# Reordering a hybrid encoder step: group A's prompt attention beside group B's projection, decode beside group B's attention, output projection 512 wide

## The chip, the cores and the metric

The kernel runs on one core of a Trainium2 chip, as one launch. The metric is the device time of that launch in microseconds. Each of the core's engines works through a queue of its own in order: TensorE (PE, matmuls and transposes; weight loads are PEld), VectorE (DVE), ScalarE (ACT), GpSimd (POOL) and SyncE (SP, which here issues every DMA). They wait for each other by semaphores.

## The reference

One layer of an encoder, for a prompt of 1024 tokens and for 8 decode sequences of 16 new tokens with caches. Half of the 16 heads (group A) use stick-breaking attention over the whole past, half (group B) softmax attention over a band of 8 chunks of 64 with a relative bias.

```python
def stick_breaking(q, k, v, q_pos, k_pos):
    z = jnp.einsum('bqhd,bkhd->bhqk', q, k).astype(jnp.float32) * (HEAD_DIM ** -0.5)
    causal = k_pos[None, :] < q_pos[:, None]
    log_keep = jnp.where(causal, jax.nn.log_sigmoid(-z), 0.0)
    between = lax.cumsum(log_keep, axis=3, reverse=True) - log_keep
    w = jnp.where(causal, jnp.exp(jax.nn.log_sigmoid(z) + between), 0.0)
    return jnp.einsum('bhqk,bkhd->bqhd', w.astype(v.dtype), v)

def trunk_layer(x, p, ...):
    h = rmsnorm(x, g_mix)
    q_a, k_a, v_a, q_b, k_b, v_b = split_heads(h, w_in)
    ...
    a = rmsnorm(a, g_out_sb.reshape(N_HEADS_SB, HEAD_DIM))
    o_b = rmsnorm(o_b, g_out_cb.reshape(N_HEADS_CB, HEAD_DIM))
    mix = jnp.concatenate([a.reshape(b, t, W_SB), o_b.reshape(b, t, W_CB)], axis=-1)
    x = x + mix @ w_out
    h = rmsnorm(x, g_ffn)
    x = x + (jax.nn.silu(h @ w_gate) * (h @ w_up)) @ w_down
    gate = jax.nn.sigmoid(rmsnorm(x, g_ple) @ w_ple_gate)
    x = x + gate * (p @ w_ple_proj)
    return x, new
```

The model width is 1024, a head has 64 dimensions, the past is 1024 tokens for group A and 512 for group B in decode. All data are float32. The new keys and values are outputs too.

## The kernel before

**Precision and tiles.** A float32 operand is split into a high and a low part in a reduced type: ACT copies the high part, and DVE (or POOL, where the source is in SBUF) subtracts it for the low part (`sub`, L108). A product is then three matmuls, `mm3` (L103 to L106). Prompt and decode tokens form nine tiles of 128 rows, eight for the prompt and one for the 128 decode tokens.

**Stages.** The program is written as generators, each `yield` being one step, and `advance(main, side, ratio, steps)` runs a main generator with `ratio` steps of a side one after each of its own. `schedule_with_timeline_sim` then orders the instructions on each engine. The order in the program is its priority, so an instruction that finds its inputs and a buffer free can be placed ahead of earlier ones.

1. The norm and transposes of x give `hT`.
2. `qkv_group(0)` (L211): group A's k, v and q by w_in, six weight chunks in 48 steps; the results go to DRAM (`qkT`, `vhl`) and to the outputs.
3. `qkv_group(1)` beside `decode` at 0.8 decode steps a step.
4. `attention` over eight head pairs, four of group A and then four of group B. A unit is one head and one tile of 128 queries: `scores` (L537), five units later `flip` (transposes the weights, L576), one further `outputs` (L597), and after each pair `finish` (L622). That makes 64 units for each group. For group A, `scores` has two sigmoids on ACT, a scan on DVE (L569) and a product on POOL (L570). Beside the first 64 units run `embed` (L751, the per-layer embedding, 18 steps) at 0.5 and decode at 0.4; beside the next 48, decode at 0.7; beside the rest, `half_out` at 1.5.
5. `half_out` (L828): `mix` (L807) loads group A's attention output back from DRAM and transposes it, then the first 512 rows of w_out are applied, 256 columns at a time. `lower` (L870) applies group B's half together with the next norm.
6. The feed-forward part, the per-layer gate and the final norm.

**Decode.** There are 16 batches (8 sequences, group A and then group B), with 4 chunks of 256 past tokens for group A and 2 for group B, each once for k and once for v: 96 steps and one to set up. A chunk of 512 KB is loaded into a raw tile `draw` (L131 to L134), of which there are two (`RAWS`). `fetch(i + 2)` is asked for once step i is under way and needs a raw tile that is free again. A k chunk is transposed by PE (L367) and split by ACT (L369) and DVE; a v chunk is copied by ACT (L148) and subtracted by POOL (L109), and the raw tile is free when the last reader has ended.

**Buffers.** PSUM has eight banks. In stages 1 to 3 the right side holds decode's (`d` = 2, `a` = 1), the left side `t` = 2, `o` = 2 and `s` = 1; in stage 4 the left side has `s` = 2 and `t` = 3. `half_out`'s `m` = 2 takes the place of `d` and `a`, after decode. Weights go through `Chunks`, one raw tile (`wraw`) and two pairs (`whi`, `wlo`); attention's tiles for q, k and v carry these same tags, and `finish` uses `wraw`.

Of the kernel before, what the change touches and what calls it, by code (L numbers as in the profile page):

```python
# [13 lines left out]
F32 = mybir.dt.float32  # L14
F32R = mybir.dt.float32r
# [7 lines left out]
P = 128  # L23
D = 1024
KT = 8
NP = 8
NT = 9
HD = 64
# [4 lines left out]
N4, SKEW = 14, 3  # L33
LAG, RAWS, PT = 5, 2, 2


@with_exitstack
def tile_hymba_step(
# [172 lines left out]
    def qkv_group(grp, ch, hT, stg, pso, pst):  # L211
        def parts(n, src, scale=1.0):
            hl = [stg.tile([P, 384], F32R, name=f"st{x}", tag=f"st{x}")[:, :n] for x in "hl"]
# [13 lines left out]
        for i, (w, c) in enumerate(order):  # L227
# [16 lines left out]
                for g in range(3):  # L244
# [14 lines left out]
                    else:  # L259
                        sv = stg.tile([P, 12, 2, HD], F32R, name="sv", tag="sv", bufs=1)  # L260
                        flat = st.rearrange("p t (h d) -> p (t h) d", d=HD)
                        A.copy(sv[:, :, 0, :], flat)
                        sub(G, sv[:, :, 1, :], flat, sv[:, :, 0, :])
                        nc.sync.dma_start(
                            vhl[grp][c, g * 384 : (g + 1) * 384, :].rearrange("(t p) n -> p t n", p=P),
                            sv.bitcast(F32).rearrange("p (t h) x d -> p t (h x d)", t=3),
                        )
# [230 lines left out]
    def attention(qp, ap_, ps, lag):  # L498
# [7 lines left out]
        def head(st, hh):  # L506
# [5 lines left out]
            qk = qp.tile([P, 2 * D], F32R, name="qk", tag="whi", bufs=2)  # L512
            vk = qp.tile([P, 2 * D], F32R, name="vk", tag="wlo", bufs=2)
# [16 lines left out]
        def bias(st, hh):  # L530
            toep = ap_.tile([P, (7 + hh) * P], F32, name="toep", tag=f"keep{2 + hh}")[:, :640]
# [5 lines left out]
        def scores(st, hh, t):  # L537
# [6 lines left out]
            if not grp:  # L544
                keep = ap_.tile([P, (5 + t % 4) * P], F32, name="keep", tag=f"keep{t % 4}")[:, :n]
# [51 lines left out]
        def outputs(st, hh, g, wt):  # L597
# [20 lines left out]
            tmp = ap_.tile([P, 256], F32, name="obt", tag="obt", bufs=2)  # L618
# [174 lines left out]
    for _ in dec:  # L793
        pass
# [245 lines left out]
```

## Time and profile before

| | us |
|---|---|
| median of 3 runs | 1923.72 |
| lowest and highest run | 1920.15, 1925.52 |
| the profiled execution | 1920.99 |
| its span, first to last instruction | 1919.2 |
| PE busy in it | 1833.9 (96%) |
| PEld busy | 1733.7 (90%) |
| DVE, POOL, ACT busy | 823.2, 722.3, 718.2 |
| mean granted TensorE clock | 0.991 |

The profile is of one execution. Its page gives the busy time of each engine, then the span in 40 equal slices of 48 us, where a digit is the busy share in tenths. Tables by stage give, for a stretch A:B, its length and the busy time and number of instructions of each engine, followed by the granted TensorE clock, the busy share of the DMA engines and GB/s. Rows by line or tile give an engine's operation, out<-in, its count, the least, median and greatest duration in ns, and the first and last start. A timeline row gives start and duration in us, and in brackets the idle time before it and what ended it. Matmuls overlap in the pipeline, so a busy PE isn't yet a PE at its peak; the distance between the starts of two matmuls is the better measure.

### The profile page before, as it was taken

To read this page: it belongs to the slowest core of one execution; us is meant where nothing else is said; L and a number is where in the kernel's file an instruction comes from. 1 tells how busy PE (TensorE), PEld (TensorE's weight loads), DVE (VectorE), ACT (ScalarE), POOL (GpSimd) and SP (SyncE) were. 2 spreads that over 40 slices of the span, in tenths; PEclk is the share of its full clock that TensorE was granted. 3 is DMA by queue.
4 is the path that set the end of the run, shared out by engine and by line. 5 is a ranking of instruction groups with operands and counts; after the bars stand their busy time and mean duration, and the time that the engine had idled before them with its cause. 6 is when DMAs were issued, how large, how long until landed. Compare 5 with 4: busy or idle time off the path is not lost.

```text
span 1919.2 us, 30012 instructions
## 1 busy us (share of the span) xinstructions
PE 1833.9 (96%) x11998; PEld 1733.7 (90%) x11998; DVE 823.2 (43%) x1590; ACT 718.2 (37%) x1545; POOL 722.3 (38%) x600
## 2 busy tenths in 40 slices
PE   7999999988888798899999999999999999999998
PEld 7999999987777688889999999999999999999898
DVE  5201332347888888783541331321322312313735
ACT  5322444347778687872241111111111111121532
POOL 4232345446567744523022223223223223122355
PEclk9999999999999899999999999999999999999999
DMA  6555556576558576773011111111111101111133
GB/s 214 201 176 177 183 192 203 172 229 184 161 144 218 150 223 196 214 234 117 12 45 45 44 44 44 44 45 44 45 44 44 44 29 38 44 45 44 36 98 132
DMA packets 166011, 220.60 MB, mean 115 GB/s; under 512 B 14576, under 2 KB 118768, under 8 KB 165872
## 3 DMA queue, kind: packets, MB, share of 16 engines
q1 hardware_dynamic: 165872, 218.69, 37.2%
q8 instruction: 95, 1.56, 0.4%
q14 instruction: 44, 0.36, 0.1%
HBM read 168.84 MB, written 49.81 MB: 114 GB/s over the span
## 4 chain that ended last, share of the span: by engine, by line
PE 61%; DVE 5%; DMA 3%; ACT 3%; POOL 2%; issue 1%; SPq 0%; POOLq 0%; ACTq 0%; DVEq 0%
PE ps L104 16%; PE ps L105 16%; PE ps L106 16%; PE acc L104 2%; PE acc L106 2%; DVE keep L569 2%; PE acc L105 2%; DMA draw<-in_cache_cb_v 1%; PE pt L589 1%; DVE wtl L109 1%; PE pt L613 1%; PE pt L187 1%; PE pt L612 1%; PE pt L367 1%; ACT dhi L148 1%
## 5 line engine op out<-in xcount | busy, mean ns | idle before, releaser
L109 POOL TENSOR_TENSOR wlo<-wraw,whi 128x1024 fp32r<-128x1024 f32 (+1 forms) x118 | 257.2, 2200 | 605.1 <-ACT whi L148 605.1
L106 PE MATMUL ps<-hUh,wlo 128*128 128x384 f32 x1056 | 352.9, 334 | 0.0
L104 PE MATMUL ps<-hUh,whi 128*128 128x384 f32 x1056 | 352.9, 334 | 0.0
L105 PE MATMUL ps<-hUl,whi 128*128 128x384 f32 x1056 | 352.9, 334 | 0.0
L148 ACT CAST whi<-wraw 128x1024 fp32r<-128x1024 f32 (+1 forms) x118 | 107.6, 962 | 328.0 <-PE ps L106 227.4
L923 DVE TENSOR_TENSOR x<-x,ps 128x512 f32<-128x512 f32 x198 | 135.9, 687 | 158.3 <-PE ps L106 158.3
L104 PEld LDWEIGHTS ps<-hUh,whi 128*128 128x128 f32 x1056 | 198.2, 188 | 0.4
L105 PEld LDWEIGHTS ps<-hUl,whi 128*128 128x128 f32 x1056 | 198.2, 188 | 0.4
L106 PEld LDWEIGHTS ps<-hUh,wlo 128*128 128x128 f32 x1056 | 198.2, 188 | 0.0
L104 PE MATMUL ps<-whi,hTh 128*128 128x256 f32 x576 | 165.4, 287 | 0.7 <-ACT sth L215 0.6
L105 PE MATMUL ps<-wlo,hTh 128*128 128x256 f32 x576 | 164.6, 286 | 1.0 <-POOL wlo L109 1.0
L106 PE MATMUL ps<-whi,hTl 128*128 128x256 f32 x576 | 165.0, 287 | 0.0
L109 POOL TENSOR_TENSOR dlo<-draw,dhi 128x1024 fp32r<-128x1024 f32 x48 | 117.8, 2455 | 102.1 <-ACT dhi L148 95.3
L105 PE MATMUL ps<-wlo,acth 128*128 128x512 f32 x396 | 156.2, 394 | 0.0
L104 PE MATMUL ps<-whi,acth 128*128 128x512 f32 x396 | 155.3, 392 | 0.0
L106 PE MATMUL ps<-whi,actl 128*128 128x512 f32 x396 | 153.8, 388 | 0.0
L909 DVE TENSOR_TENSOR tmp<-sg,ps 128x384 f32<-128x384 f32 x66 | 36.6, 555 | 235.4 <-PE ps L106 235.4
L907 DVE TENSOR_TENSOR sg<-tmp,ps 128x384 f32<-128x384 f32 x66 | 36.5, 554 | 197.7 <-ACT tmp L906 197.7
L109 POOL TENSOR_TENSOR actl<-tmp,acth 128x384 fp32r<-128x384 f32 x66 | 66.5, 1007 | 133.8 <-ACT acth L910 133.8
L105 PEld LDWEIGHTS ps<-wlo,hTh 128*128 128x128 f32 x576 | 111.0, 193 | 1.3 <-POOL wlo L109 1.3
L104 PEld LDWEIGHTS ps<-whi,hTh 128*128 128x128 f32 x576 | 111.0, 193 | 1.1 <-ACT sth L215 0.8
L569 DVE TENSOR_TENSOR_SCAN keep<-keep,zero 128x128 f32<-128x128 f32 (+3 forms) x64 | 105.7, 1658 | 14.1 <-ACT keep L561 11.0
(187 smaller groups left out, 4439.4 us busy)
## 6 DMA issues: line engine op xcount, KB each, us to landing
draw<-in_cache_sb_k SPq DMA_DIRECT2D x32, 512.0 KB, 4.4
draw<-in_cache_sb_v SPq DMA_DIRECT2D x32, 512.0 KB, 3.9
wraw<-in_w_in SPq DMA_DIRECT2D x12, 1024.0 KB, 5.5
wraw<-in_w_gate SPq DMA_DIRECT2D x11, 1024.0 KB, 5.4
wraw<-in_w_up SPq DMA_DIRECT2D x11, 1024.0 KB, 5.5
wraw<-in_w_down SPq DMA_DIRECT2D x11, 1024.0 KB, 4.9
v<-sv SPq DMA_DIRECT2D x12, 768.0 KB, 4.1
x<-in_x_prompt SPq DMA_DIRECT2D x16, 512.0 KB, 6.4
```

Source lines behind the costliest of these rows:

```text
L104: T.matmul(out, lhsT=ah, rhs=bh, start=start, stop=False)
L105: T.matmul(out, lhsT=ah, rhs=bl, start=False, stop=False)
L106: T.matmul(out, lhsT=al, rhs=bh, start=False, stop=stop)
L109: eng.tensor_tensor(out, a, hi.bitcast(F32), op=ALU.subtract)
L148: A.copy(h[:, o], v[:, o])
L187: T.transpose(pt[:, j * P : (j + 1) * P], h[:, c : c + P], ident)
L367: T.transpose(pt[:, pr * P : (pr + 1) * P], raw[:, m, pr * P : (pr + 1) * P], ident)
L569: V.tensor_tensor_scan(rev, rev, zero[:, 0:1].to_broadcast([P, n]), 1.0, op0=ALU.mult, op1=ALU.add)
L589: T.transpose(pt[:, (c - c0) * P : (c - c0 + 1) * P], w[:, c * P : (c + 1) * P], ident)
L907: V.tensor_tensor(out[0][:, f, s], t_, ps, op=ALU.mult)
L909: V.tensor_tensor(t_, sg[:, f, s], ps, op=ALU.mult)
L923: V.tensor_tensor(x1[t][:, o], x1[t][:, o], ps, op=ALU.add)
```

## The change

Stage 2 stays. Group A's attention now runs beside `qkv_group(1)`, at `QA` = 1.2 of its steps a projection step. Decode starts after that projection, since its pool `dA` and its banks now take the right side that the projection has left, and runs beside the next 48 attention steps at `DEC` = 2.0, with `embed` at 0.4. What is then left of attention runs with `half_out` at `OUT` = 1.0.

```diff
-N4, SKEW = 14, 3
+SKEW = 3
 LAG, RAWS, PT = 5, 2, 2
+QA, DEC, OUT = 1.2, 2.0, 1.0
...
-    banks(right, "right", d=2, a=1)
-    banks(left, "left", t=2, o=2, s=1)
+    banks(left, "left", s=2, t=3)
+    banks(right, "right", o=3)
     ch = Chunks(pool(ctx, "w1", "left"), "w", 2048, 1, 2)
-    hp = pool(left, "h1", "left")
-    stg = pool(left, "stg", "left", 2)
+    hp = pool(right, "h1", "right")
+    stg = pool(right, "stg", "right", 2)
...
+    at = pool(left, "at", "left")
+    att = attention(ch.pool, at, ps, LAG)(range(8))
+
+    advance(qkv_group(1, ch, hT, stg, ps["o"], ps["t"]), att, QA)
+    right.close()
     dstack = ExitStack()
+    banks(dstack, "right", d=2, a=1)
     dp = pool(dstack, "dA", "right")
     dec = decode(Chunks(dp, "d", 1088, RAWS, 2, 1024), dp)
-    advance(qkv_group(1, ch, hT, stg, ps["o"], ps["t"]), dec, 0.8)
-
-    left.close()
-    banks(left, "left", s=2, t=3)
-    at = pool(left, "at", "left")
-    att = attention(ch.pool, at, ps, LAG)(range(8))
...
     pj = embed()
-    advance(both(att, pj, 4, 0.5), dec, 0.4, 4 * 2 * NP)
+    advance(both(att, pj, 0, 0.4), dec, DEC, 48)
     for _ in pj:
         pass
-    pstack.close()
-    advance(att, dec, 0.7, 48)
     for _ in dec:
         pass
+    pstack.close()
     dstack.close()
-    right.close()
...
     side = half_out()
-    advance(att, side, 1.5, N4)
-    w_b = [upper(ch, 0, 512)]
-    advance(att, side, 1.5)
+    advance(att, side, OUT)
     left.close()
```

The output projection works on 512 columns throughout, and its weights all come through `ch`; the pool `wA` is gone:

```diff
-        for c in range(4):
-            wh, wl = wp.load(w_out[0, :512, c * 256 : (c + 1) * 256].rearrange("(k p) c -> p k c", p=P), 4, 256)
+        for c in range(2):
+            wh, wl = out_weights(0, c)
...
-                acc = ps["m"].tile([P, 256], F32, name="acc", tag="M")
+                acc = ps["m"].tile([P, 512], F32, name="acc", tag="M")
...
+    def out_weights(grp, c):
+
+        return ch.load(w_out[0, grp * 512 : grp * 512 + 512, c * 512 : (c + 1) * 512].rearrange("(k p) c -> p k c", p=P),
+                       4, 512)
...
-    w_b += [upper(wp, c, 256) for c in (2, 3)]
+    w_b = [out_weights(1, c) for c in range(2)]
...
-        for n, w in (((512, w_b[0]),), ((256, w_b[1]), (256, w_b[2])))[half]:
-            o = slice(0, 512) if n == 512 else slice(256 * (w is w_b[2]), 256 * (w is w_b[2]) + 256)
-            for k in range(4):
-                mm3(acc[:, o], *hT.tok(t, 4 + k), w[0][:, k], w[1][:, k], k == 0, k == 3)
+        for k in range(4):
+            mm3(acc, *hT.tok(t, 4 + k), w_b[half][0][:, k], w_b[half][1][:, k], k == 0, k == 3)
```

Since attention's tiles and the projection's now live at the same time, buffers are cut or moved: attention's q, k and v get tiles of their own in `at`, and v's split is stored a token tile at a time.

```diff
-            hl = [stg.tile([P, 384], F32R, name=f"st{x}", tag=f"st{x}")[:, :n] for x in "hl"]
+            hl = [stg.tile([P, 384], F32R, name=f"st{x}", tag=f"st{x}", bufs=1 + (x == "h"))[:, :n] for x in "hl"]
...
-                        sv = stg.tile([P, 12, 2, HD], F32R, name="sv", tag="sv", bufs=1)
...
+                        for o in range(3):
+                            sv = stg.tile([P, 4, 2, HD], F32R, name="sv", tag="sv", bufs=2)
...
-            qk = qp.tile([P, 2 * D], F32R, name="qk", tag="whi", bufs=2)
-            vk = qp.tile([P, 2 * D], F32R, name="vk", tag="wlo", bufs=2)
+            qk = ap_.tile([P, 2 * D], F32R, name="qk", tag="qk", bufs=2)
+            vk = ap_.tile([P, 2 * D], F32R, name="vk", tag="vk", bufs=2)
...
-                keep = ap_.tile([P, (5 + t % 4) * P], F32, name="keep", tag=f"keep{t % 4}")[:, :n]
+                keep = ap_.tile([P, (7, 8, 6)[t % 3] * P], F32, name="keep", tag=f"keep{t % 3}")[:, :n]
...
-            tmp = ap_.tile([P, 256], F32, name="obt", tag="obt", bufs=2)
+            tmp = ap_.tile([P, 256], F32, name="obt", tag="obt", bufs=1)
```

`bias` in group B's attention takes its tile from two of the three keep tags, `embed` loads w_ple_proj as one chunk through `ch` in place of two through a pool of its own, and the program reserves less memory for dynamic DMA descriptors (`dynamic_dma_scratch_size=1024`).

More of the change, by code (lines that the diff above doesn't have):

```diff
@@ L259, in qkv_group @@
                     else:
-                        sv = stg.tile([P, 12, 2, HD], F32R, name="sv", tag="sv", bufs=1)
[L261 to L267, printed above, removed]
+                        for o in range(3):
+                            sv = stg.tile([P, 4, 2, HD], F32R, name="sv", tag="sv", bufs=2)
+                            flat = st[:, o].rearrange("p (h d) -> p h d", d=HD)
+                            A.copy(sv[:, :, 0, :], flat)
+                            sub(G, sv[:, :, 1, :], flat, sv[:, :, 0, :])
+                            tok = slice((g * 3 + o) * P, (g * 3 + o + 1) * P)
+                            nc.sync.dma_start(vhl[grp][c, tok, :], sv.bitcast(F32).rearrange("p h x d -> p (h x d)"))
                     first = 4 if grp else 0
@@ L530, in bias @@
         def bias(st, hh):
-            toep = ap_.tile([P, (7 + hh) * P], F32, name="toep", tag=f"keep{2 + hh}")[:, :640]
+            toep = ap_.tile([P, (8 - hh * 2) * P], F32, name="toep", tag=f"keep{1 + hh}")[:, :640]
             nc.sync.dma_start(toep, rel[st["pr"] * 2 + hh])
@@ L751, in embed @@
     def embed():
-        wc = Chunks(pp, "p", 1024, 1, 2)
-        wj = [wc.load(w_ple_proj[0][:, c * 512 : c * 512 + 512].rearrange("(k p) c -> p k c", p=P), 2, 512)
-              for c in range(2)]
+        wj = ch.load(w_ple_proj[0].rearrange("(k p) c -> p k c", p=P), 2, D)
         for t in range(NT):
@@ L801, in tile_hymba_step @@
     mp = pool(dstack, "mp", "right", 2)
-    wp = Chunks(pool(dstack, "wA", "right"), "w", 1024, 1, 2)
     banks(dstack, "right", m=2)
```

9 lines of the change are left out of this document (4 added, 5 removed).

## The prediction

> **What bounds the kernel now.** I read the page first, then a table of stages cut where the work changes.
>
> ```profile
> span 1919.2 us, 30012 instructions
> PE   7999999988888798899999999999999999999998
> DVE  5201332347888888783541331321322312313735
> PEclk9999999999999899999999999999999999999999
> ```
>
> TensorE is near full before slice 8 and after slice 18. Only between, where VectorE shows 7 and 8, does it fall back.
>
> ```profile
> core 0: us, PE busy (x) PEld busy (x) DVE busy (x) ACT busy (x) POOL busy (x), PEclk, DMA share, GB/s
> 186.00:412.00 226.00, 225.93 (x1781) 225.45 (x1779) 74.61 (x119) 88.09 (x171) 95.09 (x93) 1.00 0.58 186
> 412.00:668.00 256.00, 209.91 (x1435) 180.24 (x1434) 212.18 (x276) 187.26 (x447) 175.08 (x134) 0.96 0.65 179
> 668.00:816.00 148.00, 134.21 (x1052) 127.37 (x1051) 119.25 (x426) 121.24 (x304) 72.09 (x100) 0.97 0.74 208
> 816.00:872.00 56.00, 52.02 (x391) 46.52 (x391) 42.24 (x140) 38.21 (x100) 11.49 (x11) 0.99 0.67 200
> 872.00:975.00 103.00, 102.43 (x754) 96.25 (x753) 50.50 (x90) 33.03 (x57) 28.97 (x25) 1.00 0.23 70
> 975.00:1919.20 944.20, 935.65 (x5314) 885.65 (x5312) 279.74 (x467) 189.78 (x357) 284.34 (x192) 1.00 0.15 50
> ```
>
> These stages are: group B's projection with 38 decode steps; group A's 64 attention units with about 26 decode steps and the embedding; group B's units with the rest of decode; the tail of attention with the half output projection; the output projection; and the feed-forward part, which nothing touches. The unit counts come from the scan (one per A unit) and the negated maximum (one per B unit):
>
> ```profile
> L569 DVE TENSOR_TENSOR_SCAN keep<-keep,zero x64: 392/1696/3595, 413.8 to 660.4; 128x128 f32<-128x128 f32 x8, 128x256 f32<-128x256 f32 x8, 128x384 f32<-128x384 f32 x8, 128x512 f32<-128x512 f32 x8
> L572 DVE TENSOR_SCALAR mxp<-mxp x49: 94/145/154, 668.5 to 816.0; 128x1 f32<-128x1 f32 x49
> L572 DVE TENSOR_SCALAR mxp<-mxp x17: 97/144/154, 815.9 to 847.4; 128x1 f32<-128x1 f32 x17
> ```
>
> So an A unit takes 4.0 us (256/64) at 83% VectorE busy, and a B unit 3.0 us beside decode. Attention is vector-bound while the projection before it leaves VectorE two thirds idle. That is what the new order uses.
>
> **The change part by part.** TensorE's cost goes by pitch, start to start; busy overlaps itself.
>
> ```profile
> 169.77 0.33 PE L104 MATMUL ps<-hTh,whi 128*128 128x384 f32 x1
> 169.95 0.33 PE L105 MATMUL ps<-hTl,whi 128*128 128x384 f32 x1
> 940.19 0.39 PE L104 MATMUL acc<-whi,hUh 128*128 128x512 f32 x1
> 940.42 0.39 PE L105 MATMUL acc<-wlo,hUh 128*128 128x512 f32 x1
> 940.99 0.28 PE L105 MATMUL acc<-wlo,hUh 128*128 128x256 f32 x1
> 941.11 0.28 PE L106 MATMUL acc<-whi,hUl 128*128 128x256 f32 x1
> 942.78 1.04 PE L187 MATMUL pt<-ident,hrow 128*128 128x128 f32 x8
> ```
>
> Pitches: 0.175 us at 384 columns, 0.23 at 512, 0.12 at 256, about 0.1 for a transpose.
>
> *Output projection 512 wide.* Of the w_out products, 36 + 18 accumulators of 12 matmuls are 256 wide: 648 x 0.12 = 77.8 us. They become 324 x 0.23 = 74.5: -3.3 us. Four additions a token tile become two of twice the width, off the path.
>
> *First projection without decode.* Before 186 us, 24 of decode's transposes had been moved forward (row below); they go: -3 us. Group B's projection, stage X, then begins at 183.
>
> *Stage X: A's attention beside B's projection.* The projection is 864 matmuls x 0.12 + 288 x 0.175 + 36 transposes = 157 us. QA = 1.2 against 48 steps places 57 of the 64 A units here. By the code an A head has 4,608 key columns scored twice (at 0.45 ns a column, 4.2 us), 36 transposes (3.6) and 40 output matmuls (4.6): with masks and closing transposes about 104 us for 8 heads, 1.6 a unit. 57 of them, less the outputs that lag, are 83: 240 us together. Vector work fits under it: A's stage held VectorE for 212 us, ScalarE for 187 and POOL for 175, decode and embedding included. The new waits on fewer buffers (tmp of L618, the low half of L214, three keep tiles for four) fall on engines with that slack, and the five units of lag cover 20 us. What is queued behind them (the next sigmoid on ScalarE, the next scan on VectorE) serves TensorE only five units on. I take 10 us of TensorE waits, so 250 and an end at 433. Bounds: 0, as in 186 to 412 where TensorE never paused, to +41, the 46 idle us of A's stage times 57/64. On SP, A's seven loads a head (L516, L520) now stand among w_in's loads and the projection's stores, where a store that waits for its copy holds them back; they are asked for at a head's unit 3, some 18 us before use, which covers it. Bytes fall: 8 heads x 2 MB replace 38 cache loads of 0.5 MB. Finish's tile osb shares wraw with w_in, three times in X; a weight load is due only at the end of a chunk of some 45 us. The sv stores, 36 instead of 12 and a third as large, add 24 issues of 0.4 us on SP. If this cover went, the price would be in the +41.
>
> *Stage Y: 48 units, 96 decode steps, 18 embedding steps.* Decode's pools take the space of the projection's right side, so no raw cache tile can be loaded before 433. I allow 10 us for the eight loads on SP that stand ahead of it (constants, bias, the new q, k and v) and the release. Then two raw tiles must carry 96 loads of 512 KB one after the other. (The embedding's weights come in one load instead of two, behind A's work; that costs nothing.) What a load costs now:
>
> ```profile
> L133 SPq DMA_DIRECT2D draw<-in_cache_cb_k x5: 367/379/779, 703.9 to 741.5; - x5
> L148 ACT CAST dhi<-draw x5: 1041/1048/1070, 705.2 to 743.5; 128x1024 fp32r<-128x1024 f32 x5
> L109 POOL TENSOR_TENSOR dlo<-draw,dhi x5: 2376/2398/2406, 706.3 to 744.9; 128x1024 fp32r<-128x1024 f32 x5
> L133 SPq DMA_DIRECT2D draw<-in_cache_cb_v x5: 367/373/766, 708.7 to 747.9; - x5
> ...
> DMA to landing us min/median/max: 3.2/5.0/7.1
> ```
>
> Four intervals of V loads last 39.2 us, four of K loads 37.6: a pair in 9.6 us, 4.8 a load. It is a closed loop, as POOL and SP show together:
>
> ```profile
> 726.12 2.40 POOL L109 TENSOR_TENSOR dlo<-draw,dhi 128x1024 fp32r<-128x1024 f32 x1 [3.91 <-ACT dhi L148]
> 734.49 2.39 POOL L109 TENSOR_TENSOR dlo<-draw,dhi 128x1024 fp32r<-128x1024 f32 x1 [2.11 <-ACT dhi L148]
> ```
>
> ```profile
> 728.55 0.37 SPq L133 DMA_DIRECT2D draw<-in_cache_cb_v  x1
> 736.91 0.37 SPq L133 DMA_DIRECT2D draw<-in_cache_cb_v  x1
> ```
>
> POOL ends at 728.52, SP issues the next V load at 728.55; again 736.88 and 736.91. The tile is busy for landing, copy and subtraction, and over 668 to 809 two engines already ran into the landing:
>
> ```profile
>   ACT dhi L148: 8.4, 5
>   PE pt L367: 3.7, 3
> ...
> DMA to landing us min/median/max: 3.2/4.3/7.7
> ```
>
> With the median landing and no queueing a V loop is 4.3 + 1.05 + 2.4 + 0.3 of handing on = 8.0 us, 4.0 a load if K and V keep their own tile. The new order wants 2 loads in a B unit, where before there were 0.7, so the loop, not the ratio DEC, sets the pace. Between 4.0 (nothing queues) and 4.8 (queues as full as then) I take 4.4: engines are emptier but not empty. First load 443, last 95 x 4.4 = 418 later, 8 to finish: decode ends at 869. The bounds are 4.0 and 4.8, 38 us to either side.
>
> The double-buffering rule stands against this price: the Trainium skill, Trainium Kernel Development and Optimization, Best Practices, says to double-buffer so that DMA and compute overlap. By it two tiles would hide the transfers and the first rival would hold; the 8.4 us that ScalarE waited say it holds only at a slower pace.
>
> A rule would make the loop longer. The Trainium skill, SBUF — State Buffer, Who interferes with whom, says a VectorE instruction with two SBUF inputs and a GpSimd one that reads SBUF block each other wholly. By it the scans and products of Y could hold each subtraction up; the trace has
>
> ```profile
> L109 POOL TENSOR_TENSOR dlo<-draw,dhi x48: 2351/2394/4375, 216.8 to 813.8; 128x1024 fp32r<-128x1024 f32 x48
> ```
>
> a median 2% above the minimum, and an estimate from the one long case (2 us on a few of 48) would add under 10 us.
>
> *After decode.* The order on each engine is not strictly the program's:
>
> ```profile
> L367 PE MATMUL pt<-ident,draw x24: 270/272/273, 58.7 to 160.8; 128*128 128x128 f32 x24
> L816 SPq DMA_DIRECT2D mixn<-mixp x24: 359/372/1879, 583.3 to 918.2; - x24
> L821 PE MATMUL pt<-ident,mixn x64: 270/272/329, 829.5 to 932.0; 128*128 128x128 f32 x64
> ```
>
> Decode's transposes ran 100 us ahead of their place, mix's loads 230 us. So I expect B's last 25 units in Y's idle time, all but done at 869. What cannot come forward is half_out: its accumulators take decode's banks. Decode's end to the first mixn transpose took 13 us (816 to 829.5); then 12 mixes, 20 us with little beside them; 18 accumulators x 12 x 0.23 = 50; the group B half, another 50, with TensorE's share of the norm transposes and half 4 to 7 hidden or 1: 134 us, to 1003. If B's units are not ahead, they add up to 25 x 2 us (17 units in 31.5 us above), less the 8 in mix's gaps: +42. A single weight pool (w_gate waits for a w_out tile) costs 0 to 5, hidden by the last three token tiles.
>
> Sum: feed-forward starts at 1003 instead of 975, +28. That is against the profiled execution's 1920.99 us (span 1919.2 and 1.8 around it), 2.7 below the median of the runs: 1949.
>
> **The rivals.** *Decode is bound by engines, not by its tiles* (ends on the other side). A B unit alone is 2 us, so a decode step was 1.5 (148 - 49 x 2 = 50 over 33 steps at the old ratio), and with as much for an embedding step an A unit is 3 (256 - 26 x 1.5 - 18 x 1.5 = 190 over 64). By these 41 B units, 7 A units, 96 decode and 18 embedding steps make Y 274; with 26 for mixing them, 300. Decode ends at 743 and 25 units, half_out and the rest need 159 + 20 - 3 = 176 (159 is 816 to 975): feed-forward at 919, 1865 us. For it: by these rates no engine of Y would be as full as in the A stage. Against: the closed loop and the the landings that engines waited for. It decides once a load takes less than 4.1 us: 1949 - 95 x 0.3 = 1920.
>
> *A's chain is not hidden in X.* ScalarE copies the projection's accumulators in order with A's sigmoids, and TensorE stalls on three banks. Price +31 over my 10: 1980. Against: 187 x 57/64 + 88 = 255 us of ScalarE, less 64 decode steps in these two rows at a copy of 1.05 or more, is under 190 of 250.
>
> *Nothing runs ahead,* so that B's 25 units follow decode: +42, 1991. Against: the rows of mix above. That the change would not do what it says, decode beginning earlier, is excluded by memory it shares.
>
> **How the numbers follow.** Forecast, loop-bound decode: 0.55; engine-bound: 0.27; unhidden X: 0.08; nothing ahead: 0.10. About 0.3% (6 us) is what a measurement tells from no change. The forecast alone spans 1911 to 1987 (loads of 4.0 to 4.8 us); a tenth of that lies below 1918 and a seventh within 6 us of the median: faster 0.27 + 0.06, same 0.08, slower 0.59. With the upper half of the engine-bound case and the slower rivals up to nothing ahead, the range is 1870 to 1992.
>
> **What would show it.** Right: first cache load near 443, loads every 4.2 to 4.6 us, POOL's subtraction ending at the next V load's issue, TensorE under 75% busy in Y, over 95% before 430; first wide accumulator near 900. Wrong: loads under 4.1 us, or decode ending before 800; X longer than 280; B's units still running 40 us after decode.

## The result, and the profile after

The changed kernel takes **2008.17 us** (median of 4, 2002.41 to 2012.37) against 1924.03 us (1920.15 to 1925.52): a ratio of 1.0439, 95% interval 1.0407 to 1.047. It was forecast slower, but by 25 us instead of 84, and the time lies outside the range. The profiled execution took 2012.37 us, span 2010.6 and 1.8 around it; it was the longest of the four, 4.2 us above their median. From its page:

```profile
span 2010.6 us, 29520 instructions
...
PE 1861.2 (93%) x11674; PEld 1740.9 (87%) x11674; DVE 818.2 (41%) x1572; ACT 781.2 (39%) x1601; POOL 717.6 (36%) x616
...
PE   7999999987767778888999999999999999999998
...
PEclk9999999998888898999999999999999999999999
```

The dent starts at the same place but holds 7s and a 6 where before held mostly 8s. Beside the busy 1833.9 of 1919.2 us of before, TensorE is busy for 27.3 us more, though it issues 324 matmuls less, and idle for 64.1 us more (149.4 against 85.3): together the 91.4 us between the two spans. PEclk shows a run of 8s in the dent.

The stages of after (columns: stretch and its length, busy time and count of each engine, granted clock, DMA share, GB/s):

```profile
core 0: us, PE busy (x) PEld busy (x) DVE busy (x) ACT busy (x) POOL busy (x), PEclk, DMA share, GB/s
...
183.00:433.00 250.00, 244.83 (x1862) 235.45 (x1862) 149.06 (x198) 148.73 (x353) 122.64 (x90) 0.99 0.47 139
...
443.00:893.00 450.00, 338.67 (x2294) 307.29 (x2293) 240.22 (x579) 295.81 (x584) 200.85 (x239) 0.89 0.60 176
893.00:945.00 52.00, 45.69 (x305) 38.73 (x304) 43.96 (x154) 40.97 (x107) 9.73 (x10) 0.97 0.79 236
945.00:997.00 52.00, 52.00 (x259) 43.37 (x257) 17.19 (x32) 8.16 (x16) 9.95 (x6) 1.00 0.09 25
997.00:1020.00 23.00, 17.93 (x81) 13.38 (x80) 6.77 (x12) 10.10 (x16) 9.33 (x4) 0.85 0.46 149
1020.00:1064.00 44.00, 44.00 (x216) 36.73 (x215) 27.85 (x44) 16.00 (x30) 9.99 (x12) 1.00 0.15 48
```

Stage X, 183 to 433, is what the order was to buy: TensorE 98% busy, VectorE from the 75 us of before in the projection to 149. Stage Y, the row from 443, loses it: TensorE is busy for 339 of 450 us at a clock of 0.89, and no other engine for more than 296. TensorE's longest waits in it (what waited and what ended it, us in all, times, the longest):

```profile
PE pt L589 <- ACT w L573: 28.2, 19, 4.1
PE po L461 <- DVE own L458: 16.0, 7, 5.4
PE pt L367 <- DMA draw<-in_cache_sb_k: 14.1, 6, 6.0
PE pt L383 <- POOL wn L430: 12.5, 4, 5.3
```

The first is for group B's weights, an exponential on ScalarE; the third is for a cache chunk; the second and the fourth are inside a decode batch, for its finished output (`own`) and for its weights of the new tokens (`wn`), which come behind the scan and the product.

In Y these groups of instructions ran (count, busy time and mean of one):

```profile
L573 ACT ACT_TABLE_LOAD x21 | 26.9, 1283 | 0.4
...
L400 ACT ACT_TABLE_LOAD x20 | 25.7, 1283 | 0.4
...
L572 DVE TENSOR_SCALAR mxp<-mxp 128x1 f32<-128x1 f32 x44 | 6.5, 147 | 0.5
```

ScalarE loads a function table 41 times, 52.6 us in all (the last figure of a row is the idle time ahead of it). In before the same two lines loaded one each:

```profile
L400 ACT ACT_TABLE_LOAD x1 | 1.3, 1283 | 0.0
L573 ACT ACT_TABLE_LOAD x1 | 1.3, 1283 | 0.0
```

The reason is the new neighbour. Decode's group A uses a sigmoid (L400); before, it ran beside group A's attention, which uses a sigmoid too. Now it runs beside group B's attention, whose weights are an exponential (L573). On ScalarE's timeline (start, length, operation) the two take turns:

```profile
600.52 1.28 ACT L573 ACT_TABLE_LOAD   x1
601.81 0.40 ACT L573 ACTIVATE w<-w,mxp 128x128 f32<-128x128 f32 x1
...
609.21 1.28 ACT L400 ACT_TABLE_LOAD   x1
610.50 0.39 ACT L400 ACTIVATE wdec<-sdec 128x256 f32<-128x256 f32 x1
```

Table load, 128x128 exponential of 0.40 us, another exponential and copies, table load, sigmoid of 0.39 us: each load takes over three times as long as the activation behind it. The maxima (L572) show that 44 of group B's 64 units began in Y. The cache loads by source, and POOL's subtraction, each with its durations in ns and its first and last start:

```profile
L110 POOL TENSOR_TENSOR dlo<-draw,dhi x47: 2340/2376/4454, 470.6 to 891.4; 128x1024 fp32r<-128x1024 f32 x47
L134 SPq DMA_DIRECT2D draw<-in_cache_sb_k x32: 367/379/912, 443.4 to 727.5; - x32
...
L134 SPq DMA_DIRECT2D draw<-in_cache_cb_v x16: 367/376/539, 775.4 to 890.6; - x16
```

The first is issued at 443.4 and the last at 890.6, 95 intervals of **4.71 us**. In the last part POOL and SP show the closed loop of the prediction again, POOL first:

```profile
828.30 2.38 POOL L110 TENSOR_TENSOR dlo<-draw,dhi 128x1024 fp32r<-128x1024 f32 x1 [3.65 <-ACT dhi L149]
...
836.34 2.39 POOL L110 TENSOR_TENSOR dlo<-draw,dhi 128x1024 fp32r<-128x1024 f32 x1 [4.06 <-ACT dhi L149]
```

```profile
830.71 0.37 SPq L134 DMA_DIRECT2D draw<-in_cache_cb_v  x1
...
838.77 0.37 SPq L134 DMA_DIRECT2D draw<-in_cache_cb_v  x1
```

POOL's subtraction ends at 830.68 and SP issues at 830.71; then 838.73 and 838.77. The loop is 8.06 us, and two loads leave in it, of which the other is a k chunk's.

### The profile page after: what moved, and what is told of

It is laid out like the page before. It is cut to its first block, busy times and chain, and to the rows that moved or that the text cites. A ratio compares the mean times of both kernels' runs of the same rounds, so it can differ in the third digit from the quotient of the medians.

```text
span 2010.6 us, 29520 instructions
## 1 busy us (share of the span) xinstructions
PE 1861.2 (93%) x11674; PEld 1740.9 (87%) x11674; DVE 818.2 (41%) x1572; ACT 781.2 (39%) x1601; POOL 717.6 (36%) x616
## 4 chain that ended last, share of the span: by engine, by line
PE 75%; DMA 10%; ACT 6%; DVE 3%; POOL 3%; issue 2%; SPq 1%; POOLq 0%; ACTq 0%; DVEq 0%
PE ps L105 20%; PE ps L106 20%; PE ps L107 20%; DMA draw<-in_cache_cb_v 3%; PE pt L589 2%; POOL dlo L110 2%; DMA draw<-in_cache_sb_v 2%; DMA draw<-in_cache_sb_k 2%; PE pt L613 1%; ACT dhi L149 1%; PE pt L612 1%; PE pt L367 1%; PE acc L105 1%; PE acc L107 1%; PE acc L106 1%
## 5 line engine op out<-in xcount | busy, mean ns | idle before, releaser
L110 POOL TENSOR_TENSOR wlo<-wraw,whi 128x1024 fp32r<-128x1024 f32 (+1 forms) x114 | 264.9, 2347 | 583.8 <-ACT whi L149 583.7
L570 POOL TENSOR_TENSOR w<-w,keep 128x127 f32<-128x127 f32 (+3 forms) x64 | 82.1, 1286 | 129.0 <-DVE keep L569 113.1
L589 PE MATMUL pt<-ident,w 128*128 128x128 f32 x528 | 90.6, 291 | 37.7 <-ACT w L573 28.2
L569 DVE TENSOR_TENSOR_SCAN keep<-keep,zero 128x128 f32<-128x128 f32 (+3 forms) x64 | 99.6, 1556 | 59.6 <-ACT keep L561 59.2
L110 DVE TENSOR_TENSOR wtl<-pt,wth 128x512 fp32r<-128x512 f32 (+1 forms) x192 | 94.6, 515 | 58.3 <-ACT wth L593 56.8
```

The source lines that it names most:

```text
L110: eng.tensor_tensor(out, a, hi.bitcast(F32), op=ALU.subtract)
L569: V.tensor_tensor_scan(rev, rev, zero[:, 0:1].to_broadcast([P, n]), 1.0, op0=ALU.mult, op1=ALU.add)
L570: G.tensor_tensor(w[:, : n - 1], w[:, : n - 1], keep[:, 1:], op=ALU.mult)
L589: T.transpose(pt[:, (c - c0) * P : (c - c0 + 1) * P], w[:, c * P : (c + 1) * P], ident)
```

## The experiments

All ratios are against the kernel before, which was timed again beside each group of runs; the edits are against the kernel after, unless they say otherwise. "A load" is the interval over the 95 cache loads, "last load" its issue, "FFN" the first matmul of the feed-forward part, all from the profiled execution.

| run | us | ratio, 95% interval | a load | last load | FFN | table loads |
|---|---|---|---|---|---|---|
| before | 1924.03 | 1 | | 808.8 | 974.5 | 4 |
| after | 2008.17 | 1.0439 (1.0407 to 1.047) | 4.71 | 890.6 | 1063.5 | 44 |
| e1, 3 raw tiles | 1984.16 | 1.0312 (1.0296 to 1.0327) | 4.29 | 852.0 | 1034.5 | 46 |
| e2, 4 raw tiles | 1970.03 | 1.0239 (1.0221 to 1.0257) | 4.10 | 836.1 | 1020.6 | 44 |
| e3, subtraction on VectorE | 1995.24 | 1.0376 (1.0355 to 1.0398) | 4.38 | 858.9 | 1040.0 | 44 |
| e4, all units beside decode | 2019.96 | 1.0497 (1.048 to 1.0514) | 4.87 | 905.5 | 1069.4 | 54 |
| e5, tanh | 1993.31 | 1.0351 (1.0322 to 1.038) | 4.55 | 875.1 | 1044.4 | 4 |
| e6, tanh and 4 raw tiles | 1948.71 | 1.0128 (1.0106 to 1.0149) | 3.89 | 817.1 | 998.1 | 4 |
| e7, decode alone | 2092.97 | 1.0874 (1.0852 to 1.0897) | 3.98 | 823.4 | 1142.3 | 8 |
| e8, output 256 wide again | 2016.74 | 1.0489 (1.0461 to 1.0517) | 4.59 | 878.5 | 1069.1 | 44 |
| e9, half a step a unit | 2024.34 | 1.053 (1.0505 to 1.0555) | 4.59 | 880.2 | 1070.8 | 44 |
| e10, e6 and e9 | 1953.85 | 1.016 (1.0142 to 1.0177) | 3.85 | 812.6 | 1001.2 | 4 |
| e11, e10 and 60 units beside decode | 1970.4 | 1.0242 (1.0221 to 1.0263) | 4.08 | 834.1 | 1017.0 | 4 |
| e12, e7 and 4 raw tiles | 2037.16 | 1.059 (1.0565 to 1.0615) | 3.27 | 757.4 | 1081.5 | 8 |
| e13, before with 3 raw tiles | 1916.22 | 0.9965 (0.9953 to 0.9977) | | 794.3 | 966.3 | 4 |
| e14, before, output 512 wide | 1936.56 | 1.0064 (1.0047 to 1.0082) | | 822.2 | 986.3 | 4 |
| e15, e13 and e14 | 1922.06 | 1.0004 (0.999 to 1.0018) | | 795.9 | 967.1 | 4 |

One caution on reading it. The edits of e8, e9 and e14 act only after decode, yet the last load came 12 and 10 us earlier in e8 and e9 than in after, and 13 us later in e14 than in before. What moves it was not found; part may be scatter between executions, since after's four differ by 10 us and its profile is of the longest. So a shift of one stage by some 13 us between two programs is not read as the effect of an edit unless a second pair of runs or a row of the trace says the same.

**The raw tiles: e1, e2, e3.** e1 and e2:

```diff
-LAG, RAWS, PT = 5, 2, 2
+LAG, RAWS, PT = 5, 3, 2
```

```diff
-LAG, RAWS, PT = 5, 2, 2
+LAG, RAWS, PT = 5, 4, 2
```

> The changed kernel with three raw cache tiles in place of two (RAWS = 3). Theory L (the closed loop of a raw tile sets decode's pace, and with it the whole stage, since the engines' queues hold attention behind it): a tile is held some 9.3 us, so three of them allow a load every 3.1 us in place of 4.65. Then the engines take over, at about 3.3 us a load: stage Y falls from 450 us to 320 to 350, and the time to 1890 to 1920 us. Rival E (the engines in their fixed order, or the batch chain of scores, scan and product, set the pace, and the tile waits for them): the tiles fill up and wait longer, the time stays within 15 us of 2008.

> The changed kernel with four raw cache tiles. Theory L: with three tiles the loop no longer binds, so a fourth adds little, within 15 us of three tiles. Rival E: no change from 2008 with either.

The third tile takes off 24 us and the fourth 14 more: the direction of theory L, but e1 ends 64 us above the upper end that was expected, and three tiles did not end the gain. e3 leaves two tiles and shortens the time that one is held:

```diff
-                h, l = ch.parts(raw, 2, 512, 1)
+                h, l = ch.parts(raw, 2, 512, 1, V)
```

> The changed kernel with two raw tiles, but the low part of a v chunk is subtracted by VectorE in place of POOL. Theory L: the v tile is held 1.5 us or more shorter (2.4 us on POOL against about 1.1 for 1024 columns on VectorE, by its 0.69 for 512), so a pair of loads falls from 9.3 us to about 8, and stage Y by 30 to 70 us: 1940 to 1980. Rival E: VectorE gets 48 x 1.1 = 53 us more work and the time stays or rises, 2000 to 2040.

In e3 the subtraction is VectorE's:

```profile
L110 DVE TENSOR_TENSOR dlo<-draw,dhi x48: 1207/1226/1961, 470.0 to 871.1; 128x1024 fp32r<-128x1024 f32 x48
```

1.23 us instead of POOL's 2.38, and the load's interval falls from 4.71 to 4.38. The 13 us that it gains are of the size of the scatter and 15 us short of the expected 1980, but with e1 and e2 they are the third pair that says the same: easing the loop helps. But four tiles leave 4.10 us, where a loop of 8 us over four tiles would allow 2.0: something else holds decode as well. The traces show which part gave way, if each load is paired with its readers in order (us, means of the 96 loads):

| run | issue to landing | landed, waiting for the first reader | reading | tile held |
|---|---|---|---|---|
| after | 4.76 | 1.67 | 2.79 | 9.22 |
| e5, tanh | 4.74 | 1.44 | 2.70 | 8.88 |
| e7, decode alone | 4.13 | 1.14 | 2.69 | 7.96 |
| e2, 4 raw tiles | 4.82 | 8.76 | 2.87 | 16.45 |
| e12, alone, 4 raw tiles | 4.39 | 6.22 | 2.69 | 13.30 |

With two tiles half of the held time is about the interval of the loads, and a chunk is read soon after it has landed. With four it lies landed for 6 to 9 us: there the readers set the pace and no longer the transfers. What holds the readers was not tested; one candidate is the split's `dhi` and `dlo`, which have two buffers each in every run.

**The tables: e5, e6.** The weights as 0.5 tanh(z/2) + 0.5 instead of a sigmoid, the same values:

```diff
-                A.activation(w, sc, AF.Sigmoid)
+                A.activation(w, sc, AF.Tanh, scale=0.5)
...
+                V.tensor_scalar(w, w, 0.5, 0.5, op0=ALU.mult, op1=ALU.add)
```

> The changed kernel, two raw tiles, with decode's group A weights as 0.5 tanh(z/2) + 0.5 in place of the sigmoid (one more VectorE operation of 1040 columns a batch, 8 in all), so that ScalarE need not swap its function table between decode's sigmoid and group B's exponential. Theory T (the table loads set the pace while decode's group A runs beside group B's attention: 41 loads of 1.28 us in the profile of the changed kernel, each in the chain of both): the 41 loads go to 2 or 3, the first 64 cache loads go from 4.95 us each to about 4.1 as in the last 32, and the time falls by 40 to 60 us to 1950 to 1968. Theory L (only the hold of the raw tile counts): the loads' interval stays near 4.9 us and the time within 15 us of 2008.

The table loads go from 44 to 4, and the time falls by 15 us where 40 to 60 were expected. The gain stands where the two functions took turns: the first 64 loads come every 4.70 us instead of 4.95, the last 32 every 4.24 instead of 4.20. e6 is the same with four raw tiles:

> The same with four raw tiles. If both causes are real, neither hides the other: a load every 3.3 to 3.6 us, and the time 1900 to 1930, about the time of the kernel before. If table loads alone count, four tiles give less than 10 us beyond the run with two.

Against e2 the tables are worth 21 us there; against e5 the tiles 45. Each alone gives 15 and 38, both together 59: slightly more than the sum. That each wait hid part of the other would explain it and was not shown. That the two effects come twice, in two pairs of runs, sets them apart from the scatter above; against e2, too, the tables' gain lies in the first 64 loads (4.23 to 3.95 us) more than in the last 32 (3.83 to 3.75). The expected 1900 to 1930 us was missed. e6's mixing stage:

```profile
443.00:817.00 374.00, 308.36 (x2225) 286.80 (x2226) 240.82 (x561) 236.82 (x524) 198.67 (x238) 0.92 0.69 208
```

Two of TensorE's longest waits in it (e6's lines stand one further down):

```profile
PE po L462 <- DVE own L459: 16.0, 5, 5.1
PE pt L383 <- POOL wn L431: 15.4, 4, 5.5
```

The 95 intervals take 369 us instead of 447, and TensorE is busy for 82% of the stage instead of 75. The wait for group B's weights, 28.2 us in after, is 6.2; the two shown, inside a decode batch, are now nearly half of TensorE's 65.6 idle us.

**The loop by itself: e7, e12.** All of decode ahead of the rest of attention, so that no unit of group B queues on the engines; with two raw tiles and with four:

```diff
-    advance(both(att, pj, 0, 0.4), dec, DEC, 48)
-    for _ in pj:
-        pass
     for _ in dec:
         pass
+    advance(both(att, pj, 0, 0.4), iter(()), DEC, 48)
+    for _ in pj:
+        pass
```

> The changed kernel with all of decode first after group B's projection and the attention that is left only behind it, so that nothing but the last units of group A, the embedding and what the scheduler moves forward stands beside decode. Theory L says that the pace of the loads is the tile's own: 4.0 us a load or more even here (landing 4.3, copy 1.05, subtraction 2.4, handing on 0.3 for a v tile), so decode still lasts 385 us or more. Theory T: without swaps the loads fall well under 4 us, to 3.0 to 3.6, and decode lasts 290 to 350 us. The total time is longer than 2008 or near it, since attention then stands alone.

> Decode alone with four raw tiles in place of two. Theory L: the 4.0 us a load of decode alone are the tile's loop, and with four tiles the loads come at 3.0 to 3.4 us, decode's end 55 to 95 us earlier, the time 2000 to 2035. If the batch chain (scores, scan, product, transposes) sets the 4.0 us instead: over 3.8 us a load and within 20 us of 2093.

Decode's own stretch, e7 and then e12:

```profile
443.00:823.00 380.00, 259.32 (x1590) 232.11 (x1590) 158.08 (x285) 154.64 (x305) 164.31 (x207) 0.82 0.47 149
```

```profile
443.00:757.00 314.00, 221.16 (x1544) 201.39 (x1544) 153.18 (x273) 146.68 (x293) 156.09 (x202) 0.90 0.57 181
```

In e7 VectorE, ScalarE and POOL are each busy for 41 to 43% of it, TensorE for 68% at a clock of 0.82, and a load takes 3.98 us: this is the tile loop with nearly empty queues, the 4.0 that the prediction worked out as its lower bound. Two more tiles make it 3.27, within what was expected of the loads; the time is 2 us above what was. So by difference 0.7 of after's 4.71 us come of the units beside decode. Of the 1.26 us that a tile is held longer there than in e7, 0.63 are a longer landing (the DMA share of after's Y is 0.60 against 0.47) and 0.53 a longer wait for the first reader. TensorE's longest wait in e7 and e12 is again the one for `own`, 50.8 and 41.7 us, so the chain inside a batch takes part as well; no run took it away.

**The units left behind: e4, e9, e11.** e4 spreads decode over all units, so that none remains:

```diff
-    advance(both(att, pj, 0, 0.4), dec, DEC, 48)
+    advance(both(att, pj, 0, 0.4), dec, 1.2)
```

> The changed kernel with decode at 1.2 steps a unit beside all that is left of attention, so that no unit of group B is left for half_out, which then runs alone. Theory L with fixed order: decode's end stays near 893 us, since the loop sets it, and B's 25 units are done by then; after it come only the 134 us of the prediction's sum in place of 173, so the time is 1960 to 1980 us. Rival (the wait for decode is shared by all engines, so units cost time wherever they stand): decode's end moves back by 25 units of 2 us, and the time stays within 15 us of 2008.

With e4 the half output projection has no step left beside attention, so the mix of both groups shares one tile for the decode rows, which then holds the other group's rows; the amount of work is the same. The same goes for e11. e4's time stays within 15 us of after, as the rival had it. The last maximum now comes at 861.0, ahead of the last load, but that load is 15 us later, and its end:

```profile
905.00:970.00 65.00, 33.32 (x123) 23.83 (x124) 18.24 (x37) 22.11 (x42) 15.59 (x10) 0.53 0.55 180
```

From the last load to 970, when the accumulators begin to run one behind the other, TensorE works 33 of 65 us, at a clock of 0.53: the mixes alone do not fill it. The last load to FFN takes 164 us instead of 173. The 9 us won there are fewer than the 15 lost ahead. e9 gives the output projection half a step a unit, to close up the stretch of 997 to 1020 in after's stages, where TensorE is busy for 17.9 of 23 us at a clock of 0.85:

```diff
-QA, DEC, OUT = 1.2, 2.0, 1.0
+QA, DEC, OUT = 1.2, 2.0, 0.5
```

> The changed kernel with half_out at 0.5 steps a step of attention in place of 1.0, so that the last pair's finish stands ahead of half of half_out's accumulators on TensorE. Theory M (with OUT = 1.0 the finish of pair 7 stands behind nearly all of half_out, and the way of its result through DRAM into the last mixes is uncovered: 23 us from the last wide accumulator at 997 to the first of lower at 1020): that gap falls under 6 us and the time by 12 to 20 us, to 1988 to 1996. Rival (what is late is the units of group B themselves, whatever stands beside them): the gap only moves, the time stays within 6 us of 2008.

The stretch closed up (TensorE is busy for 20.6 of the 21 us from 997 to 1018), but the half projection's accumulators end 20 us later than in after, at 1016.5 instead of 996.9, and the time is 16 us above after: neither expectation held. e10 and e11 try the two orders on e6's kernel, e11 with 60 units beside decode in place of 48 (its edit against e10):

```diff
-QA, DEC, OUT = 1.2, 2.0, 0.5
+QA, DEC, OUT = 1.2, 1.6, 0.5
...
-    advance(both(att, pj, 0, 0.4), dec, DEC, 48)
+    advance(both(att, pj, 0, 0.4), dec, DEC, 60)
```

> Tanh, four raw tiles and half_out at 0.5 together. If theory M's gain is independent of the two in decode: 1948.7 less 12 to 20, 1929 to 1937. If not, 1945 to 1952.

> The same with decode at 1.6 steps a unit for 60 units in place of 2.0 for 48, so that 12 more units of group B stand beside decode. If stage Y has room for them (its busiest engine, TensorE, 80% by busy time), decode ends within 8 us of where it did and 12 units of 2 us go from behind it: 1905 to 1918, faster than the kernel before. If Y is full, decode's end moves back by as much as is gained: 1927 to 1940.

e10 gains nothing on e6, and e11 is 17 us slower than e10: the last load moves back by 21.5 us and the end follows. Twelve more units beside decode cost 21.5 us there and save 6 behind it, as e4's cost more than they saved; both of the times expected for e11 were too short.

**The output projection's width: e8, e14.** e8 goes back to accumulators of 256 columns; the weights still come through `ch`:

```diff
-                acc = ps["m"].tile([P, 512], F32, name="acc", tag="M")
+                acc = ps["m"].tile([P, 256], F32, name="acc", tag="M")
...
-        for k in range(4):
-            mm3(acc, *hT.tok(t, 4 + k), w_b[half][0][:, k], w_b[half][1][:, k], k == 0, k == 3)
+        for n in ((slice(0, 512),), (slice(0, 256), slice(256, 512)))[half]:
+            for k in range(4):
+                mm3(acc[:, n], *hT.tok(t, 4 + k), w_b[half][0][:, k, n], w_b[half][1][:, k, n], k == 0, k == 3)
```

> The changed kernel with the output projection 256 columns wide again where it was so before (group A's half, and the second half of group B's). The prediction's sum says 648 matmuls x 0.12 us against 324 x 0.23: +3 us, 2011. Rival (the single weight pool and two accumulator banks make the wide form slower than its pitch): 1995 to 2005.

It is 9 us slower than after, more than the 3 that the sum gave. e14 makes the projection of before 512 wide instead, with a pool of one pair of 512 columns for half of group A's weights and `ch` for the rest:

```diff
-    wp = Chunks(pool(dstack, "wA", "right"), "w", 1024, 1, 2)
+    wp = Chunks(pool(dstack, "wA", "right"), "w", 2048, 1, 1, 1024)
...
-                acc = ps["m"].tile([P, 256], F32, name="acc", tag="M")
+                acc = ps["m"].tile([P, 512], F32, name="acc", tag="M")
...
-    advance(att, side, 1.5, N4)
-    w_b = [upper(ch, 0, 512)]
-    advance(att, side, 1.5)
+    advance(att, side, 1.0)
+    w_b = []
...
-    w_b += [upper(wp, c, 256) for c in (2, 3)]
+    w_b += [upper(ch, c, 512) for c in range(2)]
```

> The kernel before, with the output projection alone made 512 wide: the group A half through the chunks of the projection and a pool of one pair of tiles of 512 columns, the group B half through the chunks of the projection, at one step a unit for 1.5. Theory (the edit is worth by itself what going back to 256 cost in the new order, 8.6 us): 1913 to 1918 us, feed-forward start at 965 to 970. Rival (3.3 us by the count of matmuls, given back because the weights of the group B half come later): 1920 to 1926 us.

Neither theory nor rival held: the kernel is slower than before, by 0.64%, some 12 us. Its last subtraction ends at 829.9 and FFN starts 156.4 us later, against 158.3 in before: the width is worth 2 us at its own place. From FFN to the end it takes 947.0 us instead of 944.7, which gives them back, and the 13.7 us by which the last subtraction ends later lie ahead of any edited line. So neither e8's 9 nor e14's 12 us is shown to be the width's.

**The third tile in the old order: e13, e15.** Before with `LAG, RAWS, PT = 5, 3, 1`; one buffer less for the embedding's halves makes room for the tile.

> The kernel before, with three raw cache tiles for two, and one buffer for the embedding's transposed halves to make room (PT 1). Theory (the raw tiles held decode's pace only in the new order, where decode is asked for two loads a unit): in the old order a unit asks for 0.7 loads, so the third tile takes away only the waits for landings, 8.4 us of ScalarE and 3.7 us of TensorE between 668 and 809 and the like of it ahead: 1911 to 1924 us. Rival (the old order is held by the raw tiles too): 20 us and more, as in the new order, 1900 us or less.

e13 is faster than both kernels, by 0.35% of before (interval 0.23 to 0.47%). Its two stages of attention beside decode:

```profile
412.00:668.00 256.00, 214.54 (x1463) 183.82 (x1462) 215.11 (x290) 192.12 (x456) 177.05 (x141) 0.96 0.62 175
668.00:816.00 148.00, 137.93 (x1095) 131.04 (x1094) 128.08 (x443) 123.28 (x318) 71.33 (x96) 0.99 0.78 214
```

TensorE's idle time falls from 46 to 41 us and from 14 to 10. That answers to the theory: the old order asks for 0.7 loads a unit, and its tiles held it little. e15 has e14's edit as well:

> Both edits in the kernel before. Theory: the two act in different stages and add up: 1903 to 1918 us, faster than both kernels. Rival: 1920 us or more, no gain beyond what a measurement can tell.

1922.06, no difference that can be told from before; the third tile is worth 14.5 us against e14, twice what e13 gives; both are of the size of the scatter, so the gain of e13 is sure as a time, and the tile as its cause only as far as the idle times above bear it out.

## Why the prediction was wrong

By its own sum the profiled execution compares so (us):

| term | predicted | measured |
|---|---|---|
| to the first cache load | 443 | 443.4 |
| 95 load intervals | 418 (4.4 each) | 447.2 (4.71) |
| last load to the end of its subtraction | 8 | 10.0 |
| from there to FFN | 134 | 162.9 |
| FFN to the end, and around the span | 946 | 948.9 |

**Stage X was right**: the count of 57 units (58 of A's scans had begun by 443), the cover for vector work and SP's queue. The rival that A's chain would not hide is out. That the first load came within 0.4 us is closer than the terms were: TensorE idled 5 us in X where 10 were taken, the projection's last matmul ended at 435.7 instead of 433, and the first load followed 8 us behind it where 10 were allowed.

**The interval of the loads was mis-sized, by 29 us.** The mechanism was right: e1, e2 and e3 ease the loop and gain, e7 shows its lower bound at 3.98, and the rival of a decode bound by engines is out, since decode with none of group B's units beside it (e7) still needs 378 us for its loads, where 96 steps of 1.5 us were that rival's price. The failed step is "engines are emptier but not empty", from which 4.4 was taken between 4.0 and 4.8. Emptier they were (VectorE 53% busy in Y against 81% in 668 to 816 of before, ScalarE 66 against 82), and the loads still took 4.71: busy time did not tell the wait. Nor does it show that a moved stage meets other functions on ScalarE. The table loads were there to be read: the rows of L400 and L573 with one load each, and the two activations in the code. With them removed (e5) the interval is 4.55. The Trainium skill, ScalarE: Activation LUTs, Table sets: the hidden batching unit, says that tables are loaded in sets, that the exponential and the sigmoid lie in different ones and tanh in both; the 44 and the 4 loads of e2 and e6 agree. The Trainium skill, ScalarE: Activation LUTs, What ACT_TABLE_LOAD costs, puts a load at 1283 ns, as the trace has it, and adds some 1380 ns of draining for each switch. By that section 40 switches would be an estimate of 106 us. No row here shows a drain: the exponential begins 0.01 us after the load at 600.52 ends, and the idle time ahead of all 41 loads is 0.8 us. By the load rows the 41 are 52.6 us, and e5, with one VectorE operation more a batch, shows that some 15 of these lay on the path with two raw tiles, e6 that 21 did with four. What is left of e5's 4.55 beyond e7's 3.98 divides by the table of held times, where a tile's time covers two intervals: a landing takes 0.61 us longer, the first reader comes 0.30 later. So the larger part is the landing, which the sum took at the median of 4.3 and which has a mean of 4.76 in after; why it takes longer was not tested. The term of under 10 us for blocked subtractions held: three of the 48 took 4.0 to 4.5 us, 5.4 us together above the median, and all three ran beside a product of L417 on VectorE.

**The end of decode to FFN was mis-sized, by 29 us too.** "So I expect B's last 25 units in Y's idle time, all but done at 869" failed. After 893 twenty units were still to come:

```profile
L572 DVE TENSOR_SCALAR mxp<-mxp 128x1 f32<-128x1 f32 x20 | 2.9, 144 | 0.1
```

TensorE had 111 idle us in Y, but did not use them for these units: they stand behind decode in the program, and the transposes and loads that had run ahead in before are no proof that a whole unit, on four engines, will. By the sum's own count of 41 units in Y, 23 and not 25 were left, 4 us of its price. The rival "nothing runs ahead", 1991 us, came nearest, partly by luck: it gave all 42 us to the units left behind, which cost 29, and the other 29 are the loads'. Where the 163 us went: 40 to the first wide accumulator (33 predicted), 56 for the 18 accumulators (50), and 66.6 from there to FFN (51). The last holds the 23 us from 997 to 1020, in which TensorE does half of the mixes' transposes and begins the other half's accumulators, idle for 5 us and at a clock of 0.85; the sum had the mixes hidden. That comes of the order as well: pair 7's closing work stands behind one accumulator a step, so that its store is the last of two here, and TensorE waits for the reload:

```profile
L654 SPq DMA_DIRECT2D mixp<-osb x2: 359/368/377, 932.4 to 991.4; - x2
...
1002.71 0.87 PE L817 MATMUL pt<-ident,mixn 128*128 128x128 f32 x3 [2.58 <-DMA mixn<-mixp]
```

But e4 and e9 say that filling these holes by another order does not shorten the sum: TensorE was busy for 160 of the 171 us from 893 to 1064. The units must be paid for in Y or behind it, and Y, while the loop holds it, charges as much.

**A price that was not in the sum is the clock.** The 27 us by which TensorE's busy time grew are, by an estimate, not work: busy time times the mean granted clock of the span (0.991 before, 0.972 after) is 1817 and 1809 us. One and the same form of matmul shows it, first at a clock of 0.50 (1001 to 1007.5) and then at 1.00 (1013 to 1023):

```profile
1006.69 0.63 PE L105 MATMUL acc<-whi,hUh 128*128 128x512 f32 x1
...
1020.10 0.39 PE L105 MATMUL acc<-whi,hUh 128*128 128x512 f32 x1
```

In the stretches with idle TensorE the granted clock was 0.89 (Y), 0.82 (e7) and 0.53 (e4's 65 us); in the stretches where it is full, 0.99 to 1.00. The busy share alone does not fix it: e12 has 0.90 at 70%, after's Y 0.89 at 75%. With e6 the busy time is 1839.4 us, back within 6 of before.

**The two edits priced at nearly nothing** stayed near it: the width's 3.3 us are 2 up to FFN where e14 could show it, and the single weight pool's 0 to 5 may be what is lost behind it, where 947.1 us instead of 944.7 pass to the end. e2, e6, e14 and e15 show that loss too, and e8, 256 wide through the same pool, does not (944.8); so it goes with the width, and which of the two causes it stays open.

What stays open: why e6, without table loads and with four tiles, is still 24.7 us above before. Its loads take 3.89 us, though decode alone reaches 3.27 (e12). TensorE's 16.0 and 15.4 us of waits for `own` and `wn` say that the chain inside a batch is part of it. The cut buffers of attention (three keep tiles, one `obt`) were not given back in any run either. Open as well is what shifts decode's end by some 13 us between programs that differ only behind it.

## What to carry to other kernels

Before two streams of work are put side by side, list what each asks of a shared engine in kind, not in microseconds alone: two functions of different tables in turn cost 41 loads here, and one rewritten function took them away. A stage that streams through buffers can run no faster than (landing + all readers) / buffers, and a new order that asks for more loads a unit needs its buffers counted anew; here one more was worth 24 us and two more 38, in the order that asked for less one more 7 (e13) to 14.5 (e15 against e14). And do not book later work into an engine's idle time unless the program's order puts it there.

## What was not expected of the hardware

A table load takes 1283 ns each time, and the next activation starts 0.01 us behind it. TensorE's granted clock was lower in the stretches where TensorE was partly idle, down to 0.82 over 380 us at 68% busy (e7), so a wait elsewhere also lengthens the matmuls that are left: in after by an estimate of 27 us over the whole span. It does not sink evenly: in after it is 0.50 from 475.2 to 485.4, with TensorE busy for 5.0 of 10.2 us, and 1.00 from 485.4 to 516.1, with 22.6 of 30.7. The Trainium skill, TensorE: Matmul & The Clock Gate, HAM oscillation — how this bites in real kernels, tells the same of a kernel whose TensorE waits for DMA again and again: the clock falls back in each wait. The two stretches agree as far as they go; that it falls in each wait no row here shows.
